# Two-layer trunk: FFN output blocks one by one in the first two parts, and the weight sums of a later pair queued behind a pair's second recombination

## The chip, the cores and the metric

The kernel runs on one core of a Trainium2 chip. The metric is the device time of one execution in microseconds (us). TensorE (PE) multiplies matrices into eight PSUM banks; VectorE (DVE), ScalarE (ACT) and GpSimd (POOL) do the element-wise work; SyncE (SP) issues most of the loads. PEld is TensorE's weight load, which runs beside its matmuls.

## The reference

512 tokens of width 1024 pass through two layers. A layer has a half-step SwiGLU feed-forward (FFN), a token mixer (retention in the first layer, forgetting attention in the second), a second half-step FFN and a gated per-layer embedding:

```
def swiglu(x, w_in, w_out):
    g, u = jnp.split(x @ w_in, 2, axis=-1)      # w_in: 1024 x (2*2816)
    return (jax.nn.silu(g) * u) @ w_out         # w_out: 2816 x 1024

h = h + 0.5 * swiglu(rmsnorm(h, nw[0]), ffn_w_in[i, 0], ffn_w_out[i, 0])
h = h + mixer(rmsnorm(h, nw[1]))
h = h + 0.5 * swiglu(rmsnorm(h, nw[2]), ffn_w_in[i, 1], ffn_w_out[i, 1])
h = h + sigmoid(rmsnorm(h, nw[3]) @ ple_w_gate[i]) * (p[i] @ ple_w_proj[i])
```

Everything is float32. The change touches the four FFNs alone.

## The kernel before

**Precision.** A float32 operand is split into a high part in TensorE's fp32r format and a low part, the remainder. A product takes three matmuls: high x high, high x low, low x high (lines L323, L324 and L325 for tiles of 512 tokens; L508 in `product`). For a weight block ScalarE casts the high part (L83) and VectorE subtracts for the low part (L84). For some blocks ScalarE casts and also writes the negated block (L125, L126), and a load of GpSimd's queue adds the block to it in memory (L127).

**FFN input.** A hidden block is 128 of the 2816 gate columns and the same of the up columns; there are 22 in an FFN. Most are made by a scheme of seven half-size products, on a `Pair` of weight tiles q and r of 512 KB each. r and q are added in four combinations (`emit_sums_now`, adds at L157: s1 to s4), each of which is split like a weight (tiles s12 and s34; a12 is a half of r, and `x` in the code). The pair's products go into two banks g and u:

- `one`: 24 matmuls of 128x256. `two`: 12 more, and a recombination: ScalarE copies g (L561), VectorE adds it to u (L562), ScalarE copies the sum (L564, called u2 in the code), VectorE adds that to g (L565).
- `three`: 48 matmuls. The first 12 need the copy of L564, the next 12 the sum of L565, the last 12 the a12 tile.
- `finish`: a copy (L578), two adds (L579, L580), and the gate: L585, Silu at L586, L590, and the split of the result (L313, L314) into the activation `act[m]`.

The first two or three blocks of an FFN are made without this scheme (`plain`). The others run in three parts, hidden blocks 0 to 5, 6 to 13 and 14 to 21. In a part the loop begins pair m + 1 (`start`, `one`, `two`) ahead of `three` and `finish` of pair m. At a part's end the first pair of the next part is begun; then the part's activations are multiplied with the output weights.

**FFN output.** `out_blocks` makes output blocks of 128 of the 1024 columns. Each takes 18 or 24 matmuls of 128x512 (three for each of the part's 6 or 8 hidden blocks). Then VectorE scales the bank (L604) and adds it to the residual stream `hall` (L607). Blocks 0 and 1 are made together, with their matmuls in turns; blocks 2 to 7 singly.

**What sets the order.** TensorE's order is the order of the code. A scheduler orders VectorE, ScalarE, GpSimd and SP. `issue_after` gives it one constraint: an instruction has to stand behind another one on the same engine. Weights are loaded and split ahead of use, through four raw buffers (`wraw`) and three split ones (`w8`, shown as w); the begun pair's q keeps one of the three during the output blocks. Sums are made for pairs up to two ahead of the number of pairs taken (`ahead`, `pairs_used`): before, `take_pair` counted a pair and asked for the sums at `start`.

## Time and profile before

| | |
|---|---|
| three runs, us | 2182.68, 2182.79, 2186.28; median 2182.79 |
| the profiled execution | 2182.19 us, of which the span is 2180.4 |
| DMA traffic | 268.40 MB, mean 123 GB/s |
| FFN0, FFN1, FFN2, FFN3 in the span, us | about 20 to 358, 767 to 1119, 1179 to 1505, 1761 to 2090 |

A row of a timeline has the start in us, the duration in us, engine, line, operation, output tile <- input tiles, shape and how many; in brackets the engine's idle time just before it, and the engine, tile and line whose work ended that idle time. A row of waits has the waiting engine, tile and line, what it waited for, the us in total, the number of waits and the longest. The ends of TensorE's matmuls are modelled; the distance between starts is the better measure of its pace.

### The profile page before, as it was taken

To read this page: it belongs to the slowest core of one execution; us is meant where nothing else is said; L and a number is where in the kernel's file an instruction comes from. 1 tells how busy PE (TensorE), PEld (TensorE's weight loads), DVE (VectorE), ACT (ScalarE), POOL (GpSimd) and SP (SyncE) were. 2 spreads that over 40 slices of the span, in tenths; PEclk is the share of its full clock that TensorE was granted. 3 is DMA by queue.
4 is the path that set the end of the run, shared out by engine and by line. 5 is a ranking of instruction groups with operands and counts; after the bars stand their busy time and mean duration, and the time that the engine had idled before them with its cause. 6 is when DMAs were issued, how large, how long until landed. Compare 5 with 4: busy or idle time off the path is not lost.

```text
span 2180.4 us, 34464 instructions
## 1 busy us (share of the span) xinstructions
PE 2138.2 (98%) x13537; PEld 1925.9 (88%) x13537; DVE 1446.2 (66%) x2627; ACT 1201.6 (55%) x2022; POOL 443.0 (20%) x344
## 2 busy tenths in 40 slices
PE   9999999999999999999999999999999999999997
PEld 9898987888888798989989999998788898999987
DVE  9776766352533677767758687775675686867765
ACT  8464553433333574746557565465786774655544
POOL 0010103444344000101110011012234200100055
PEclk9999999999999999999999999999999999999999
DMA  6464563222222244746526465564522144655631
GB/s 192 114 175 131 141 155 97 83 93 78 95 79 87 78 128 133 173 113 159 146 93 156 125 164 150 139 152 115 147 83 92 67 119 121 167 144 140 155 106 40
DMA packets 85603, 268.40 MB, mean 123 GB/s; under 512 B 9392, under 2 KB 12976, under 8 KB 85440
## 3 DMA queue, kind: packets, MB, share of 16 engines
q1 hardware_dynamic: 63328, 209.78, 29.0%
q0 software_dynamic: 20880, 55.32, 15.1%
q8 instruction: 106, 1.74, 0.3%
q10 hardware_dynamic: 1232, 1.09, 0.1%
q14 instruction: 57, 0.47, 0.1%
HBM read 264.02 MB, written 2.13 MB: 122 GB/s over the span
## 4 chain that ended last, share of the span: by engine, by line
PE 83%; DVE 6%; ACT 5%; DMA 3%; issue 2%; POOL 0%; SPq 0%; DVEq 0%; ACTq 0%; POOLq 0%
PE bank L508 31%; PE bank L325 14%; PE bank L323 14%; PE bank L324 14%; PE bank L543 3%; DMA wraw<-in_ffn_w_in 3%; PE bank L710 2%; PE bank L711 2%; PE bank L712 2%; DVE w L84 1%; ACT p L1014 1%; DVE tlo L314 1%; ACT w L83 1%; ACT p L1016 1%; DVE sums L157 1%
## 5 line engine op out<-in xcount | busy, mean ns | idle before, releaser
L83 ACT CAST w<-wraw 128x1024 fp32r<-128x1024 f32 (+1 forms) x238 | 241.5, 1022 | 421.6 <-PE bank L325 260.3
L325 PE MATMUL bank<-unit_a,w 128*128 128x512 f32 x736 | 287.0, 390 | 4.3 <-DVE w L84 2.6
L323 PE MATMUL bank<-unit_a,w 128*128 128x512 f32 x736 | 288.4, 392 | 1.9 <-ACT w L83 1.6
L324 PE MATMUL bank<-unit_a,w 128*128 128x512 f32 x736 | 286.7, 390 | 0.2 <-DVE unit_a L314 0.2
L83 ACT CAST s<-sums 128x512 fp32r<-128x512 f32 x316 | 189.1, 617 | 152.4 <-DVE sums L157 104.2
L325 PE MATMUL bank<-unit_d,w 128*128 128x512 f32 (+1 forms) x712 | 267.7, 376 | 4.7 <-DVE w L84 4.7
L323 PE MATMUL bank<-unit_d,w 128*128 128x512 f32 (+1 forms) x712 | 268.7, 377 | 3.2 <-ACT w L83 1.5
L324 PE MATMUL bank<-unit_d,w 128*128 128x512 f32 (+1 forms) x712 | 267.8, 376 | 1.7 <-DVE unit_d L314 1.7
L84 DVE TENSOR_TENSOR s<-sums,s 128x512 fp32r<-128x512 f32 x316 | 211.8, 686 | 75.0 <-ACT s L83 74.8
L84 POOL TENSOR_TENSOR w<-wraw,w 128x1024 fp32r<-128x1024 f32 x83 | 201.4, 2429 | 232.5 <-ACT w L83 224.0
L127 POOL DMA_DIRECT2D a<-in_ffn_w_in x80 | 70.1, 876 | 645.5 <-ACT a L126 452.4
L84 DVE TENSOR_TENSOR w<-wraw,w 128x1024 fp32r<-128x1024 f32 (+1 forms) x155 | 183.1, 1186 | 22.5 <-ACT w L83 22.3
L508 PE MATMUL bank<-unit_b,s 128*128 128x256 f32 x872 | 184.1, 277 | 1.7 <-DVE bank L565 1.7
L604 DVE SCALAR_TENSOR_TENSOR tmp<-bank,rows 128x512 f32<-128x512 f32 x96 | 66.1, 690 | 169.6 <-PE bank L325 168.3
L508 PE MATMUL bank<-unit_d,s 128*128 128x256 f32 x1140 | 178.4, 276 | 0.0
L508 PE MATMUL bank<-unit_a,s 128*128 128x256 f32 x1224 | 170.4, 276 | 0.0
L325 PEld LDWEIGHTS bank<-unit_a,w 128*128 128x128 f32 x736 | 138.2, 188 | 35.2 <-DVE w L84 4.3
L323 PEld LDWEIGHTS bank<-unit_a,w 128*128 128x128 f32 x736 | 138.2, 188 | 32.2 <-ACT w L83 3.5
L324 PEld LDWEIGHTS bank<-unit_a,w 128*128 128x128 f32 x736 | 138.2, 188 | 28.3 <-DVE unit_a L314 0.5
L325 PEld LDWEIGHTS bank<-unit_d,w 128*128 128x128 f32 x712 | 134.2, 188 | 30.5 <-DVE w L84 6.6
L323 PEld LDWEIGHTS bank<-unit_d,w 128*128 128x128 f32 x712 | 134.2, 188 | 30.1 <-ACT w L83 3.2
L324 PEld LDWEIGHTS bank<-unit_d,w 128*128 128x128 f32 x712 | 134.2, 188 | 26.3 <-DVE unit_d L314 3.2
(295 smaller groups left out, 4802.7 us busy)
## 6 DMA issues: line engine op xcount, KB each, us to landing
wraw<-in_ffn_w_in SPq DMA_DIRECT2D x174, 512.0 KB, 4.4
wraw<-in_ffn_w_out SPq DMA_DIRECT2D x64, 512.0 KB, 4.7
w<-in_ffn_w_in POOLq DMA_DIRECT2D x57, 512.0 KB, 5.4
a<-in_ffn_w_in POOLq DMA_DIRECT2D x79, 256.0 KB, 6.2
wraw<-in_ffn_w_out SPq DMA_DIRECT2D x32, 384.0 KB, 3.8
wraw<-in_ret_qk SPq DMA_DIRECT2D x16, 512.0 KB, 3.5
wraw<-in_ret_v SPq DMA_DIRECT2D x16, 512.0 KB, 3.6
wraw<-in_ret_g SPq DMA_DIRECT2D x16, 512.0 KB, 3.5
```

Source lines behind the costliest of these rows:

```text
L83: self.nc.scalar.copy(hi, raw)
L84: self.low.tensor_tensor(out=lo, in0=raw, in1=hi.bitcast(F32), op=ALU.subtract)
L127: self.nc.gpsimd.dma_start(out=lo, in_=src, accum_op=ALU.add)
L323: nc.tensor.matmul(out, wh, xh, start=first, stop=False)
L324: nc.tensor.matmul(out, wh, xl, start=False, stop=False)
L325: nc.tensor.matmul(out, wl, xh, start=False, stop=last)
L508: add = lambda w, x, start, stop: nc.tensor.matmul(out, w, x, start=start, stop=stop, skip_group_check=True)
L543: nc.tensor.matmul(o[:, HALVES[t]], x[:, ks], y, start=k == t == q == 0, stop=k == KB - 1 and q == 2, skip_group_check=True,)
L604: nc.vector.scalar_tensor_tensor(out=t1, in0=o, scalar=-0.5, in1=n.r, op0=ALU.mult, op1=ALU.mult)
L710: nc.tensor.matmul(os[t], xh, wh[:, js], start=k == 0, stop=False)
L711: nc.tensor.matmul(os[t], xh, wl[:, js], start=False, stop=False)
L712: nc.tensor.matmul(os[t], xl, wh[:, js], start=False, stop=k == KB - 1)
```

## The change

It does two things. In the first two parts of each FFN the output blocks 0 and 1 are made one after the other; in the third part they stay together. And a pair is counted, and the sums of the pair two ahead are asked for, at the end of `two` instead of at `start`, with the constraint that VectorE's first add of these sums stands behind `two`'s last VectorE instruction.

```
-    def take_pair(self, pair):
-        self.take(pair)
+    def next_sums(self, behind):
         self.pairs_used += 1
+        self.behind = (behind,)
         self.emit_sums()
-        return pair
+        self.behind = ()
...
         def start(m):
-            live[m] = W.take_pair(ins[m]), bank(), bank()
+            W.take(ins[m])
+            live[m] = ins[m], bank(), bank()
...
             nc.scalar.copy(u2, u[:, c1])
-            nc.vector.tensor_tensor(out=g[:, c1], in0=g[:, c1], in1=u2, op=ALU.add)
+            last = nc.vector.tensor_tensor(out=g[:, c1], in0=g[:, c1], in1=u2, op=ALU.add)
             live[m] += (cc,)
+            W.next_sums(last)
...
-            for ms in ((0, 1), (2,), (3,), (4,), (5,), (6,), (7,)):
+            pair = [(0, 1)] if done == NF else [(0,), (1,)]
+            for ms in pair + [(m,) for m in range(2, KB)]:
                 out_blocks(c, ms)
```

Lines move: the recombination is L562, L563, L565 and L566 in the changed kernel (L561, L562, L564, L565 before), `finish` L580, L581, L582, L587, L588 and L592 (L578, L579, L580, L585, L586, L590), the output drain L606 and L609 (L604, L607).

VectorE's order in the steady run of FFN0's third part. `sums` are the additions of a pair two ahead, `s_...` the low halves of sums; before:

```order
L157 TENSOR_TENSOR sums<-wraw 128x512
L562 TENSOR_TENSOR bank<-bank,tmp 128x256
L314 TENSOR_TENSOR unit_d<-tmp,unit_d 128x512
L84 TENSOR_TENSOR s_3052<-sums,s_3052 128x512
L84 TENSOR_TENSOR s_2782<-sums,s_2782 128x512
L565 TENSOR_TENSOR bank<-bank,tmp 128x256
L84 TENSOR_TENSOR s_2919<-sums,s_2919 128x512
L157 TENSOR_TENSOR sums<-sums,wraw 128x512
L579 TENSOR_TENSOR bank<-bank,tmp 128x256
```

The same place after:

```order
L563 TENSOR_TENSOR bank<-bank,tmp 128x256
L314 TENSOR_TENSOR unit_d<-tmp,unit_d 128x512
L566 TENSOR_TENSOR bank<-bank,tmp 128x256
L157 TENSOR_TENSOR sums<-wraw 128x512
L84 TENSOR_TENSOR s_2826<-sums,s_2826 128x512
L84 TENSOR_TENSOR s_3096<-sums,s_3096 128x512
L84 TENSOR_TENSOR s_2963<-sums,s_2963 128x512
L157 TENSOR_TENSOR sums<-sums,wraw 128x512
L581 TENSOR_TENSOR bank<-bank,tmp 128x256
```

The first add of the sums, the one that waits for a load, moved from ahead of the recombination (L562, L565 before) to behind it (L563, L566 after). ScalarE at the same place after (the copies of `two` at L562 and L565, then the negated weights of a later pair):

```order
L588 ACTIVATE tmp<-tmp 128x512
L562 COPY tmp<-bank 128x512
L313 CAST unit_d<-tmp 128x512
L565 COPY tmp<-bank 128x256
L125 CAST w_3042<-wraw 128x1024
L126 ACTIVATE w_3042<-wraw 128x1024
```

Both copies stand ahead of the weights' casts there. ScalarE at the end of FFN0's first part, where the last pair's `two` is recombined; before:

```order
L561 COPY tmp<-bank 128x512
L564 COPY tmp<-bank 128x256
L83 CAST w_934<-wraw 128x768
L313 CAST unit_d<-tmp 128x512
L83 CAST s_726<-sums 128x512
L83 CAST s_811<-sums 128x512
L578 COPY tmp<-bank 128x256
L125 CAST a_812<-wraw 128x512
L126 ACTIVATE a_812<-wraw 128x512
```

And after:

```order
L562 COPY tmp<-bank 128x512
L83 CAST s_852<-sums 128x512
L83 CAST s_853<-sums 128x512
L83 CAST w_934<-wraw 128x768
L83 CAST s_770<-sums 128x512
L313 CAST unit_d<-tmp 128x512
L83 CAST s_855<-sums 128x512
L125 CAST a_856<-wraw 128x512
L126 ACTIVATE a_856<-wraw 128x512
L565 COPY tmp<-bank 128x256
L580 COPY tmp<-bank 128x256
```

The pair's second copy (L564 before, L565 after) moved from the place right behind the first copy to behind the casts of the sums and of a12. On TensorE only the matmuls of blocks 0 and 1 change places, in the first two parts; SP and GpSimd keep their order.

## The prediction

> **What bounds the kernel now.** I read the page first, then TensorE's list of waits, then its timeline around each wait in the four FFNs, then VectorE's and ScalarE's timelines at the same places.

> The page's span and busy shares, then four rows of TensorE's waits (total us, times, longest us):

> ```profile
> span 2180.4 us, 34464 instructions
> PE 2138.2 (98%) x13537; PEld 1925.9 (88%) x13537; DVE 1446.2 (66%) x2627; ACT 1201.6 (55%) x2022; POOL 443.0 (20%) x344
> ...
> PE bank L325 <- DVE w L84: 7.3, 9, 2.0
> PE bank L508 <- ACT tmp L564: 4.1, 4, 3.0
> PE bank L323 <- ACT w L83: 3.1, 8, 0.5
> PE bank L508 <- DVE bank L565: 1.7, 1, 1.7
> ```

> TensorE works 98% of the span, and the change takes no instruction away, so it can only win TensorE's idle time: some 42 us in all, of which the four rows are the waits at the two places that the change touches. One of the nine in the first row (2.0 us) is TensorE waiting in the tail of FFN3 and stays.

> **Part 1: single output blocks in the first two parts.** TensorE's timeline after the pair (0,1), in FFN0's first part (six k-blocks) and second (eight):

> ```profile
> 87.51 0.39 PE L325 MATMUL bank<-unit_d,w 128*128 128x512 f32 x1
> 88.14 0.50 PE L323 MATMUL bank<-unit_d,w 128*128 128x512 f32 x1 [0.25 <-ACT w L83]
> 88.48 0.40 PE L324 MATMUL bank<-unit_d,w 128*128 128x512 f32 x1
> 89.55 0.51 PE L325 MATMUL bank<-unit_d,w 128*128 128x512 f32 x1 [0.67 <-DVE w L84]
> 89.89 0.40 PE L323 MATMUL bank<-unit_d,w 128*128 128x512 f32 x1
> ...
> 201.83 0.39 PE L325 MATMUL bank<-unit_d,w 128*128 128x512 f32 x1
> 202.72 0.50 PE L323 MATMUL bank<-unit_d,w 128*128 128x512 f32 x1 [0.51 <-ACT w L83]
> 203.06 0.40 PE L324 MATMUL bank<-unit_d,w 128*128 128x512 f32 x1
> 204.13 0.50 PE L325 MATMUL bank<-unit_d,w 128*128 128x512 f32 x1 [0.68 <-DVE w L84]
> 204.47 0.39 PE L323 MATMUL bank<-unit_d,w 128*128 128x512 f32 x1
> ```

> Undisturbed, one matmul follows another after 0.227 us, so four steps take 0.91. From 87.51 to 89.89 they take 2.38: 1.47 lost, of which 0.92 is idle time in brackets and 0.55 a slower start after the two waits (0.27 each). From 201.83 to 204.47 it is 1.73. The waits list has eight such places (four FFNs, two parts): 3.1 + 7.3 - 2.0 = 8.4 us idle, and 8 x 0.55 = 4.4 for the starts: **12.8 us**.

> Why they wait: VectorE and ScalarE there (two answers), with the later single blocks behind:

> ```profile
> 87.25 1.37 DVE L604 SCALAR_TENSOR_TENSOR tmp<-bank,rows 128x512 f32<-128x512 f32 x2 [6.13 <-PE bank L325]
> 88.54 1.82 DVE L84 TENSOR_TENSOR w<-wraw,w 128x768 fp32r<-128x768 f32 x2
> ...
> 93.52 0.69 DVE L604 SCALAR_TENSOR_TENSOR tmp<-bank,rows 128x512 f32<-128x512 f32 x1 [1.95 <-PE bank L325]
> ...
> 94.85 0.95 DVE L84 TENSOR_TENSOR w<-wraw,w 128x768 fp32r<-128x768 f32 x1
> 97.59 0.69 DVE L604 SCALAR_TENSOR_TENSOR tmp<-bank,rows 128x512 f32<-128x512 f32 x1 [1.79 <-PE bank L325]
> ...
> 87.25 1.57 ACT L83 CAST w<-wraw 128x768 fp32r<-128x768 f32 x2 [6.59 <-PE bank L325]
> ```

> Both blocks of the pair finish together, so both weight buffers come free together. Block 2's cast and subtraction begin only then, and VectorE first drains two banks. Blocks 3 to 7 already run alone with the same buffers: block 3 ended at 93.52, the low half of the buffer that it freed was rewritten by 94.85 + 0.95 = 95.80, and the block after next wanted it at 97.59, when block 4 ended: 1.8 us to spare. With singles, blocks 0 and 1 each have 18 matmuls (93.52 to 97.59: 4.07 us), or 24 in the second part (5.44); the cast, drain and subtraction take 2.3 us after a block by these rows (some 0.4 more at 1024 columns). So block 2's weights come over a block early: gain 12.8, bounds 0 and 12.8; I take 12.8, because those single blocks wait nowhere.

> A single block 0 reaches its last k-block sooner. The last activation's low half, and TensorE's first output matmul:

> ```profile
> 78.42 0.69 DVE L314 TENSOR_TENSOR unit_d<-tmp,unit_d 128x512 fp32r<-128x512 f32 x1 [0.69 <-ACT unit_d L313]
> ...
> 79.55 0.40 PE L323 MATMUL bank<-unit_d,w 128*128 128x512 f32 x1
> ```

> It is written at 79.11; a single block asks for it 15 matmuls after 79.55, at 82.95: 3.8 us of cover, so no cost. Nothing is added: as many matmuls, casts, drains and loads, and the SP and GpSimd queues keep their order.

> **Part 2: the weight sums behind two's second recombination.** The waits of TensorE on `two`, in all FFNs, and the granted clock after the longest (us; PE, PEld, DVE, ACT, POOL busy; PEclk):

> ```profile
> 55.85 0.85 PE L508 MATMUL bank<-unit_b,s 128*128 128x256 f32 x5 [1.69 <-DVE bank L565]
> ...
> 279.90 1.69 PE L508 MATMUL bank<-unit_a,w 128*128 128x256 f32 x12 [0.41 <-ACT tmp L564]
> 292.87 1.83 PE L508 MATMUL bank<-unit_a,w 128*128 128x256 f32 x12 [3.04 <-ACT tmp L564]
> ...
> 1045.41 0.51 PE L508 MATMUL bank<-unit_b,w 128*128 128x256 f32 x2 [0.41 <-ACT tmp L564]
> ...
> 2039.01 0.50 PE L508 MATMUL bank<-unit_b,w 128*128 128x256 f32 x2 [0.25 <-ACT tmp L564]
> ...
> 294.50:299.00 4.50, 4.50 (x28) 4.50 (x28) 4.40 (x9) 2.18 (x5) 0.87 (x1) 0.65 0.94 221
> ```

> Third parts: 0.41 + 3.04 + 0.41 + 0.25 = 4.1 idle, 4 x 0.27 for the starts, and 4.50 x (1 - 0.65) = 1.6 at the low clock: **6.8 us**. FFN0's first part: 1.69 + 0.27 = 1.96.

> The low clock is a cost of the long wait. [...] In the trace the clock was 1.00 before that wait and 0.65 after it, so the measurement decides.

> Where the third parts' waits come from (VectorE's and ScalarE's timelines; the last two rows are from the chain of waits):

> ```profile
> 264.42 0.69 DVE L157 TENSOR_TENSOR sums<-wraw 128x512 f32<-128x512 f32 x1 [3.54 <-DMA wraw<-in_ffn_w_in]
> ...
> 275.74 0.69 DVE L157 TENSOR_TENSOR sums<-wraw 128x512 f32<-128x512 f32 x1 [1.35 <-DMA wraw<-in_ffn_w_in]
> ...
> 288.72 0.69 DVE L157 TENSOR_TENSOR sums<-wraw 128x512 f32<-128x512 f32 x1 [3.02 <-DMA wraw<-in_ffn_w_in]
> 289.33 0.42 DVE L562 TENSOR_TENSOR bank<-bank,tmp 128x256 f32<-128x256 f32 x1
> ...
> 292.46 0.36 ACT L564 COPY tmp<-bank 128x256 f32<-128x256 f32 x1
> ...
> 270.40 5.21 DMA wraw<-in_ffn_w_in
> ...
> 281.71 6.89 DMA wraw<-in_ffn_w_in
> ```

> VectorE waits for the r-weights of a pair two ahead and has L562 of the pair in hand queued behind. The rounds of this loop are 11.3 us (264.42 to 275.74) and 13.0 (to 288.72): from the sum to the next load's issue 6.0 (264.42 to 270.40), then 5.2 or 6.9 to landing. A pair costs TensorE 12.97 - 3.04 - 0.27 = 9.66 us (279.90 to 292.87, 84 matmuls; so `three`'s 48 take 5.5 and `one` and `two` 4.1). The loop is longer than the pair, so VectorE falls back each round until `two` is late.

> After the change L563 to L566 stand ahead of the sum, and ScalarE's copies of `two` (L562, L565) no longer lie between sum and a12 cast. Count from T0, the end of `three` of an earlier pair. VectorE and ScalarE have the rest of that pair's `finish` and then the recombination, eight dependent steps of 0.36 to 0.69 us (rows above and below), 4.0 in sum; with a handover of 0.1 to 0.2 each and one subtraction between, L566 is done at about T0 + 5.7. `three` of the same pair starts at T0 + 4.1 + 5.5 + 4.1 = 13.7, or at T0 + 9.6 where the part ends and no further pair is begun. That leaves 4 us at the least, and the r-load, now behind the recombination, can no longer hold it in its own round. From sum to the end of the a12 cast five steps remain, some 3.3 us; with the landing 8.5 to 10.2, about the pair's 9.66, so VectorE no longer falls back by more than 0.5 us a round. Queued behind the waiting sum are now the next `finish`'s L581 and L582, which TensorE meets only two pairs later. The step that is moved issues two loads besides: r on the SP queue (512 KB, the landings above) and the accumulating load of a12 on GpSimd's. Both queues keep their order; the second feeds `three`'s last product two pairs on. The sums themselves come later by some 3 us; they are wanted a pair period later still, so that costs nothing; were that cover gone, `one` would wait instead. I take 6.8; ends: 0 (the wait only moves) and 6.8.

> FFN0's first part differs: only three pairs, and the order shows ScalarE's u2 copy (L565) behind the casts of a12 (L125, L126). TensorE and ScalarE there before:

> ```profile
> 69.87 1.60 PE L508 MATMUL bank<-unit_a,w 128*128 128x256 f32 x12
> ...
> 70.07 0.62 ACT L125 CAST a<-wraw 128x512 fp32r<-128x512 f32 x1 [0.47 <-PE bank L508]
> 70.59 0.63 ACT L126 ACTIVATE a<-wraw 128x512 fp32r<-128x512 f32 x1
> ```

> Those casts wait for the end of the `three` before and start 0.20 us after the next `three` (69.87) could. With the wait at 55.85 gone, that point is 69.87 - 1.96 = 67.91. The casts then run from 68.11 to about 69.2, the copy to 69.55, and the last pair's `three` starts at 69.6 instead of 67.9. Of the 1.96 us, 1.7 come back as a new wait, and its start: net **0.2 us** won; ends 2.0 (no new wait) and -1 (VectorE's L566 later still).

> **Sum.** 12.8 + 6.8 + 0.2 = 19.8 us. The profiled execution took 2182.19 us (span 2180.4 and 1.8 around it), 0.6 below the median of the runs, 2182.79. 2182.2 - 19.8 = 2162.4; against the median **2163.0 us**, 0.9% faster. Within 0.2% (4.4 us) I call it no change; about that is what a measurement of this kernel can tell.

> **Rivals.**
> 1. *Only the output blocks win.* The loads stay late (up to 6.9 us here), VectorE falls back as before, and the third parts wait at `finish` or at another copy. For it: the loop with a late landing (10.2) is still over the pair's 9.66, and the new order binds VectorE only, so ScalarE can still put casts first, as in FFN0's first part. Against: in the third part's order the copy L565 stands ahead of L125. 2182.8 - 12.8 - 0.2 = 2169.8.
> 2. *Only the sums win.* Single blocks wait at 0 or 1 in place of 2, since a lone block asks for its second weights after 4.1 us. Against: the 1.8 us to spare above. 2182.8 - 6.8 - 0.2 = 2175.8.
> 3. *Slower: a new wait at the end of every part.* There `three` of the last pair follows the one before with only its 5.5 us between, and what I expect in FFN0's first part (1.7 + 0.27 = 1.97) would come at all twelve ends, since VectorE reaches L566 only after a sum that a late load holds. Eleven more at 1.97 are 21.7 us: 2184.7, no change. From 2.2 us each, (19.8 + 4.4) / 11, it is slower; at the longest such wait in the trace, 3.04 + 0.27, it is 36.4 us: 2199. Against: the 4 us of slack above, against landings at most 1.7 us apart (5.2 and 6.9). [...]

> **Chances.** The forecast 0.58 (2161 to 2165, by FFN0's ends). Rival 1 0.20, since the loop is near the pair's time. Rival 2 0.08. Part-end waits: no change 0.05, slower 0.05. More than forecast (other small waits go too) 0.04. So faster 0.90, same 0.05, slower 0.05. The range 2159 to 2173 holds the forecast, rival 1 and mixtures between them.

> **What would show it.** Part 1 right: no wait of L323 or L325 on w behind block 1, and L606 of blocks 0 and 1 a block apart. Part 2 right: no wait of L508 on L565 or L566 in the third parts, no clock dip near 295, L563 at VectorE before the sum's wait for its load. FFN0: a wait of some 1.7 us on L565 near 68. Wrong if L508 waits at each part's end, or if L323 waits for w at block 1.

## The result, and the profile after

The changed kernel took 2166.36 us in the median of its first six runs, against 2181.49 us before (six runs): a ratio of 0.9932, with a 95% interval of 0.9921 to 0.9944. Two later sets beside the kernel before gave 0.9921 (0.9908 to 0.9935) and 0.9929 (0.9917 to 0.9941). Over all sets the mean of 17 runs is 2165.5 us, that of 39 runs before 2181.5: 16.0 us less (standard error 0.6), where 19.8 were forecast. The profiled execution of the changed kernel took 2164.15 us, 18.0 less than the profiled one before.

The page of the changed kernel, and the rows of TensorE's waits that answer to those of before:

```profile
span 2162.4 us, 34445 instructions
PE 2131.9 (99%) x13537; PEld 1925.9 (89%) x13537; DVE 1454.0 (67%) x2627; ACT 1205.3 (56%) x2022; POOL 444.2 (21%) x344
...
PE bank L325 <- DVE w L84: 2.0, 1, 2.0
...
PE bank L508 <- ACT tmp L565: 1.5, 1, 1.5
```

Of the four rows of before, L323's wait for w and L508's for the add are gone. L325's has one wait left, the one in FFN3's tail; L508's wait on two's second copy has gone from four places to one, and that one is new.

VectorE where blocks 0 to 2 of FFN0's first part now run singly:

```profile
83.74 0.69 DVE L606 SCALAR_TENSOR_TENSOR tmp<-bank,rows 128x512 f32<-128x512 f32 x1 [2.73 <-PE bank L325]
84.47 0.69 DVE L609 TENSOR_TENSOR hall<-hall,tmp 128x512 f32<-128x512 f32 x1
85.08 0.95 DVE L84 TENSOR_TENSOR w<-wraw,w 128x768 fp32r<-128x768 f32 x1
87.82 0.69 DVE L606 SCALAR_TENSOR_TENSOR tmp<-bank,rows 128x512 f32<-128x512 f32 x1 [1.79 <-PE bank L325]
```

Block 0 ends at 83.74, the low half for block 2 is written at 85.08 + 0.95 = 86.03, and block 2 starts when block 1 ends, at 87.82: 1.8 us to spare, where TensorE had lost 1.5 us.

VectorE in FFN0's third part, around three successive rounds:

```profile
257.42 0.42 DVE L563 TENSOR_TENSOR bank<-bank,tmp 128x256 f32<-128x256 f32 x1
258.19 0.69 DVE L314 TENSOR_TENSOR unit_d<-tmp,unit_d 128x512 fp32r<-128x512 f32 x1 [0.35 <-ACT unit_d L313]
258.80 0.42 DVE L566 TENSOR_TENSOR bank<-bank,tmp 128x256 f32<-128x256 f32 x1
259.14 0.68 DVE L157 TENSOR_TENSOR sums<-wraw 128x512 f32<-128x512 f32 x1
...
268.86 0.68 DVE L157 TENSOR_TENSOR sums<-wraw 128x512 f32<-128x512 f32 x1
...
278.59 0.68 DVE L157 TENSOR_TENSOR sums<-wraw 128x512 f32<-128x512 f32 x1
```

The rounds are 9.72 and 9.73 us, TensorE's time for a pair, where they had been 11.3 and 13.0, and no bracket stands at L157. Over the whole kernel VectorE's waits for r fell from 58.7 us to 7.8; its row before and after:

```profile
DVE sums L157 <- DMA wraw<-in_ffn_w_in: 58.7, 43, 3.5
...
DVE sums L157 <- DMA wraw<-in_ffn_w_in: 7.8, 8, 1.6
```

TensorE has no wait behind the eight that are left.

TensorE, ScalarE and VectorE at the new wait, the end of FFN0's first part:

```profile
67.89 0.28 PE L508 MATMUL bank<-unit_c,a 128*128 128x256 f32 x1
69.66 1.58 PE L508 MATMUL bank<-unit_a,w 128*128 128x256 f32 x11 [1.50 <-ACT tmp L565]
...
68.20 0.62 ACT L125 CAST a<-wraw 128x512 fp32r<-128x512 f32 x1 [0.68 <-PE bank L508]
68.72 0.62 ACT L126 ACTIVATE a<-wraw 128x512 fp32r<-128x512 f32 x1
69.25 0.35 ACT L565 COPY tmp<-bank 128x256 f32<-128x256 f32 x1
...
68.20 0.42 DVE L563 TENSOR_TENSOR bank<-bank,tmp 128x256 f32<-128x256 f32 x1
```

The copy stands behind the two a12 casts, which start when TensorE has freed their buffer at the end of the `three` before. It also needs VectorE's first add, and that came only at 68.20, behind the sums of another pair. So the casts are not all of the wait: right behind the add the copy would have ended at about 69.0 instead of 69.60 (an estimate from these rows). That is some 0.6 of the 1.76 us lost; the rest is the late add.

Both traces have all 13,537 matmuls, so each matmul's start after can be set against the same one's before. What TensorE gained, stage by stage:

| where | gained, us |
|---|---|
| after the pair (0,1), eight places | 1.50, 1.76, 1.51, 1.73, 1.49, 1.76, 1.50, 1.76; together 13.0 |
| third parts, waits on `two` and the half clock near 295 | 5.64 in FFN0, 0.67 in FFN1, 0.51 in FFN3; together 6.8 |
| FFN0's first part | 1.98 + 0.12 - 1.76 = 0.3 |
| 364 to 369 us, a half clock that before did not have | -1.63 |
| the rest (the start, a load of the forgetting attention) | about -0.5 |
| the whole span | 18.0 |

### The profile page after: what moved, and what is told of

Same layout as the page of the kernel before. It is cut to its first block, busy times and chain, and to the rows that moved or that the text cites. A ratio compares the mean times of both kernels' runs of the same rounds, so it can differ in the third digit from the quotient of the medians.

```text
span 2162.4 us, 34445 instructions
## 1 busy us (share of the span) xinstructions
PE 2131.9 (99%) x13537; PEld 1925.9 (89%) x13537; DVE 1454.0 (67%) x2627; ACT 1205.3 (56%) x2022; POOL 444.2 (21%) x344
## 4 chain that ended last, share of the span: by engine, by line
PE 89%; DVE 4%; ACT 4%; issue 2%; DMA 1%; POOL 0%; SPq 0%; DVEq 0%; ACTq 0%; POOLq 0%
PE bank L508 35%; PE bank L323 14%; PE bank L324 14%; PE bank L325 14%; PE bank L543 4%; PE bank L713 2%; PE bank L714 2%; PE bank L715 2%; ACT p L1017 1%; DVE tlo L314 1%; ACT w L83 1%; DVE w L84 1%; ACT p L1019 1%; PE bank L337 0%; DMA wraw<-in_ffn_w_in 0%
## 5 line engine op out<-in xcount | busy, mean ns | idle before, releaser
L83 ACT CAST w<-wraw 128x1024 fp32r<-128x1024 f32 (+1 forms) x238 | 242.5, 1022 | 425.2 <-PE bank L325 257.8
L323 PE MATMUL bank<-unit_a,w 128*128 128x512 f32 x736 | 288.7, 392 | 0.3 <-DVE tmp L1051 0.3
L325 PE MATMUL bank<-unit_a,w 128*128 128x512 f32 x736 | 287.1, 390 | 1.7 <-POOL w L84 1.7
L324 PE MATMUL bank<-unit_a,w 128*128 128x512 f32 x736 | 287.4, 390 | 0.2 <-DVE unit_a L314 0.2
L83 ACT CAST s<-sums 128x512 fp32r<-128x512 f32 x316 | 185.7, 618 | 159.6 <-PE bank L508 89.5
L323 PE MATMUL bank<-unit_d,w 128*128 128x512 f32 (+1 forms) x712 | 268.2, 377 | 1.6 <-DVE unit_b L317 0.6
L324 PE MATMUL bank<-unit_d,w 128*128 128x512 f32 (+1 forms) x712 | 267.6, 376 | 1.8 <-DVE unit_d L314 1.8
L325 PE MATMUL bank<-unit_d,w 128*128 128x512 f32 (+1 forms) x712 | 267.1, 375 | 2.0 <-DVE w L84 2.0
L84 DVE TENSOR_TENSOR s<-sums,s 128x512 fp32r<-128x512 f32 x316 | 208.8, 686 | 65.8 <-ACT s L83 65.0
L84 POOL TENSOR_TENSOR w<-wraw,w 128x1024 fp32r<-128x1024 f32 x83 | 202.6, 2444 | 232.7 <-ACT w L83 222.6
L84 DVE TENSOR_TENSOR w<-wraw,w 128x1024 fp32r<-128x1024 f32 (+1 forms) x155 | 183.6, 1185 | 27.5 <-ACT w L83 27.4
L508 PE MATMUL bank<-unit_b,s 128*128 128x256 f32 x872 | 183.1, 276 | 0.0
L508 PE MATMUL bank<-unit_d,s 128*128 128x256 f32 x1140 | 178.3, 276 | 0.0
L606 DVE SCALAR_TENSOR_TENSOR tmp<-bank,rows 128x512 f32<-128x512 f32 x96 | 66.1, 689 | 164.5 <-PE bank L325 163.2
L508 PE MATMUL bank<-unit_a,s 128*128 128x256 f32 x1224 | 170.0, 276 | 0.0
L325 PEld LDWEIGHTS bank<-unit_a,w 128*128 128x128 f32 x736 | 138.6, 188 | 31.2 <-POOL w L84 2.1
L323 PEld LDWEIGHTS bank<-unit_a,w 128*128 128x128 f32 x736 | 138.5, 188 | 29.5 <-DVE tmp L1051 0.5
L324 PEld LDWEIGHTS bank<-unit_a,w 128*128 128x128 f32 x736 | 138.6, 188 | 28.6 <-DVE unit_a L314 0.5
L323 PEld LDWEIGHTS bank<-unit_d,w 128*128 128x128 f32 x712 | 134.0, 188 | 27.0 <-ACT unit_d L313 1.4
L325 PEld LDWEIGHTS bank<-unit_d,w 128*128 128x128 f32 x712 | 134.1, 188 | 26.3 <-DVE w L84 2.2
L324 PEld LDWEIGHTS bank<-unit_d,w 128*128 128x128 f32 x712 | 134.1, 188 | 26.3 <-DVE unit_d L314 3.2
```

Source lines behind the costliest of these rows:

```text
L83: self.nc.scalar.copy(hi, raw)
L84: self.low.tensor_tensor(out=lo, in0=raw, in1=hi.bitcast(F32), op=ALU.subtract)
L323: nc.tensor.matmul(out, wh, xh, start=first, stop=False)
L324: nc.tensor.matmul(out, wh, xl, start=False, stop=False)
L325: nc.tensor.matmul(out, wl, xh, start=False, stop=last)
L508: add = lambda w, x, start, stop: nc.tensor.matmul(out, w, x, start=start, stop=stop, skip_group_check=True)
```

## The experiments

Gains below called "by TensorE's starts" are read in the same way, matmul against matmul. Times of different sets are compared with the kernel before in the same set.

**The changed kernel again.** No edit.

> The changed kernel once more, timed beside the kernel before and profiled anew. Its first profile has the eight waits after the pair gone (13.0 us by TensorE's starts, instruction against instruction), 6.8 us gone in the third parts, 0.3 in FFN0's first part, and 1.6 us lost again at 364 to 369 us, where TensorE ran at half clock after an unchanged wait of 1.70 us that had cost no clock before. Theory A: the clock dips by chance of phase after waits of 1.5 to 3 us, so the same kernel shows other dips in another execution; expected here: 14 to 19 us below the kernel before, and at 364 a dip or none. Theory B: the dip at 364 belongs to the changed kernel (what runs ahead of it decides); expected: a dip of 1.6 us at the same place again.

Ratio 0.9921 (0.9908 to 0.9935), median 2165.15 against 2183.03 us. The profile repeats every stage of the first to 0.4 us except the clock. The granted clock behind the unchanged wait near 364 (stretch, PE, PEld, DVE, ACT and POOL busy, PEclk, DMA share, GB/s), in the first profile:

```profile
358.00:363.50 5.50, 4.19 (x18) 2.95 (x17) 3.20 (x4) 2.00 (x2) 2.02 (x1) 1.00 0.00 0
364.40:368.40 4.00, 4.00 (x12) 3.10 (x12) 3.29 (x3) 1.21 (x2) 2.23 (x1) 0.57 0.59 178
```

and in the second, with the wait itself:

```profile
363.77 0.50 PE L325 MATMUL bank<-unit_a,w 128*128 128x512 f32 x1 [1.71 <-POOL w L84]
...
364.20:368.20 4.00, 4.00 (x19) 3.29 (x18) 3.38 (x4) 1.12 (x2) 2.32 (x1) 1.00 0.61 160
```

The wait is the same (1.70 and 1.71 us), the program is the same, and only one execution dips. Theory B, a dip that belongs to the changed kernel, falls. The mean granted clock of this execution was 0.998, against 0.996 in the first, which had a second dip, in FFN3's tail (from 2092.06 us, 1.5 us lost). It is 3.1 us shorter than the first, as much as the first's two dips cost.

**Only the single blocks.** The kernel before, with the new `pair` lines alone:

```
-            for ms in ((0, 1), (2,), (3,), (4,), (5,), (6,), (7,)):
+            pair = [(0, 1)] if done == NF else [(0,), (1,)]
+            for ms in pair + [(m,) for m in range(2, KB)]:
```

> Only the output blocks 0 and 1 singly in the first two parts; the sums asked for at start as before. Theory A (two independent parts): TensorE's starts show the eight waits gone, 13.0 us, and the waits at 55.85 and in the third parts as before (some 1.9 and 6.8 us); the time falls by 13 us, give or take 3 for clock dips. Rival: the single blocks also bring the loads forward, so that the third parts' waits shrink with them; then 15 to 20 us. Other rival: without the moved sums the wait goes to blocks 0 and 1; then under 6 us.

0.9941 (0.9928 to 0.9955), which is 12.9 us (9.8 to 15.7) of the 2183.03 of before in this set. By TensorE's starts the same eight gains, 1.49 to 1.76, 13.0 together, so the wait did not go to blocks 0 and 1. The waits on `two` stay, but not in their old sizes:

```profile
55.69 0.50 PE L508 MATMUL bank<-unit_b,s 128*128 128x256 f32 x2 [1.13 <-DVE bank L565]
...
286.67 1.58 PE L508 MATMUL bank<-unit_a,w 128*128 128x256 f32 x11 [0.92 <-ACT tmp L564]
...
1036.84 0.51 PE L508 MATMUL bank<-unit_b,w 128*128 128x256 f32 x2 [1.36 <-ACT tmp L564]
```

The one of 3.04 us in FFN0 is now 0.92; FFN1's grew from 0.41 to 1.36. One profile could not tell an effect of the single blocks from chance; the last experiment but one does.

**Only the moved sums.** The changed kernel with the old line of blocks, the edit above the other way round.

> Only the sums behind the second recombination; blocks 0 and 1 as a pair everywhere. Theory A: the waits on the copy and the add of two go in the third parts (6.8 us with the half clock near 295), 0.3 us net in FFN0's first part with a new wait of 1.5 us near 69, and the eight waits after the pair stay: 7 us below the kernel before, give or take 3 for clock dips. Rival: part of the third parts' gain came from the single blocks' earlier loads; then 1 to 5 us.

0.9978 (0.9967 to 0.999), which is 4.8 us (2.2 to 7.2). By TensorE's starts 6.8 us in the third parts and 0.3 in FFN0's first part, against the profile of before, with the eight waits after the pair unchanged:

```profile
PE bank L325 <- DVE w L84: 7.3, 9, 2.0
PE bank L323 <- ACT w L83: 3.1, 8, 0.5
...
PE bank L508 <- ACT tmp L565: 1.5, 1, 1.5
```

The two parts add up: 12.9 + 4.8 = 17.7 us, and both together gave 17.2 in the same set. The single blocks' 12.9 is what their profile says; the sums' 4.8 is under the 6.8 + 0.3 of theirs, though its interval just reaches it. It lies in the rival's 1 to 5 us as well. Against the rival speaks this profile, in which no wait on `two` is left in the third parts though the blocks run as a pair, and the next profile of the kernel before, below.

**FFN0's sums one pair later.** In `two`, for FFN0 alone, the sums asked for after pair 4 wait until after pair 5:

```
-            W.next_sums(last)
+            if i or m != 4:
+                W.next_sums(last)
+            if not i and m == 5:
+                W.next_sums(last)
```

> The changed kernel, but in FFN0's first part the sums of pair 6 (asked for after two of pair 4) are asked for only after two of pair 5, together with those of pair 7. Theory A: the new wait of 1.5 us at 69.7 exists because ScalarE's copy L565 of pair 5 stands behind the casts of pair 6's a12, which wait for a buffer that TensorE frees only at 68; with the sums later the copy is ahead of them and TensorE saves 1.7 us there, so 1.5 to 2 us below the changed kernel by TensorE's starts. Rival: the copy is late because VectorE is full there (L563 at 68.2 behind eight subtractions and adds); then the wait stays or comes back at one of pair 6, and the gain is under 0.5 us.

0.9906 (0.9891 to 0.9921), median of four runs 2161.74 us. TensorE gains 1.76 us at 70 us and keeps it through the FFNs; for a load of the forgetting attention it waits 2.1 us, against 1.4 in the changed kernel. VectorE and ScalarE there:

```profile
62.66 0.43 DVE L563 TENSOR_TENSOR bank<-bank,tmp 128x256 f32<-128x256 f32 x1 [0.76 <-PE bank L508]
...
63.13 0.37 ACT L565 COPY tmp<-bank 128x256 f32<-128x256 f32 x1 [0.57 <-DVE bank L563]
...
68.11 0.62 ACT L125 CAST a<-wraw 128x512 fp32r<-128x512 f32 x1 [0.93 <-PE bank L508]
```

The copy is done 4.6 us before the casts, and the wait is gone. But the run does not tell theory from rival: with the sums later, VectorE came to the first add at 62.66, where it had been 68.20. In the changed kernel both were late, the add because of the sums ahead of it on VectorE, the copy because of the casts.

**No constraint.** The sums asked for at the end of `two`, but free on VectorE:

```
-        self.behind = (behind,)
         self.emit_sums()
-        self.behind = ()
```

> The changed kernel with the sums still asked for at the end of two, but without the constraint that binds them behind two's last VectorE instruction. VectorE's order then has the waiting sum between L563 and L566 instead of behind L566; ScalarE's order is the same. Theory A: in the changed kernel VectorE waits nowhere for a load of r (43 waits and 58.7 us before, none after), since the loop of sum, casts and next load has become shorter than a pair; so a sum ahead of L566 costs nothing and the time is that of the changed kernel within 1.5 us by TensorE's starts (clock dips left out). Rival: it is the constraint that keeps late loads out of two's way; then waits of L508 on L565 or L566's lines come back in the third parts, 2 us or more.

0.9913 (0.9896 to 0.9929), median 2162.6 us. TensorE waits nowhere on `two`, in the third parts or at 70 us, where the 1.76 us are gained too. VectorE does wait for r again; a round, and the row of its waits (line numbers from L196 on are two lower in this kernel):

```profile
265.65 0.42 DVE L561 TENSOR_TENSOR bank<-bank,tmp 128x256 f32<-128x256 f32 x1
266.93 0.69 DVE L157 TENSOR_TENSOR sums<-wraw 128x512 f32<-128x512 f32 x1 [0.85 <-DMA wraw<-in_ffn_w_in]
267.54 0.68 DVE L312 TENSOR_TENSOR unit_d<-tmp,unit_d 128x512 fp32r<-128x512 f32 x1
268.14 0.43 DVE L564 TENSOR_TENSOR bank<-bank,tmp 128x256 f32<-128x256 f32 x1
...
DVE sums L157 <- DMA wraw<-in_ffn_w_in: 30.7, 37, 2.5
```

Theory A had it right that a sum ahead of the last add costs nothing, though not that VectorE would wait nowhere: it waits 30.7 us in 37 places, all of them covered (in the changed kernel 7.8 us in 8, not none). Nor is ScalarE's order the same. At the end of FFN0's first part the first add, the copy and the a12 cast are:

```profile
64.60 0.42 DVE L561 TENSOR_TENSOR bank<-bank,tmp 128x256 f32<-128x256 f32 x1
...
65.64 0.35 ACT L563 COPY tmp<-bank 128x256 f32<-128x256 f32 x1
...
68.45 0.62 ACT L125 CAST a<-wraw 128x512 fp32r<-128x512 f32 x1 [0.20 <-PE bank L506]
```

The gain of the third parts thus comes with the place in the program at which the sums are asked for, which lets the scheduler put L561 (the first add) and ScalarE's copies ahead of them; the constraint adds nothing there. In FFN0's first part the new wait comes with it: without it the add runs 3.6 us earlier and the copy ahead of the casts.

**The pair at 2 and 3.**

```
-            pair = [(0, 1)] if done == NF else [(0,), (1,)]
-            for ms in pair + [(m,) for m in range(2, KB)]:
+            blocks = ((0, 1), (2,), (3,)) if done == NF else ((0,), (1,), (2, 3))
+            for ms in blocks + ((4,), (5,), (6,), (7,)):
```

> The changed kernel with blocks 2 and 3 made together in the first two parts, in place of 0 and 1 before. Theory A (a pair asks for two weight buffers at once and frees two at once): two disturbances at each of the eight places, a wait for block 3's weights just after the pair starts (block 1's buffer comes free only then: cast, drain and subtraction of 2.3 us, less what TensorE can do with block 2: 1.5 to 2 us), and one like before's at block 4 (1.5 or 1.7 us): 25 to 30 us more than the changed kernel. Rival (the wait belongs to the start of the output stage, where loads and the last activations come late): single blocks 0 and 1 have passed that, so the pair costs under 5 us in all.

2197.12 us in one run. By TensorE's starts it lost, at each of the eight places, twice what the old pair lost once: 3.0 or 3.6 us, 26.4 together (in the rest to 33 are the clock, with a mean of 0.994 against 0.996, and a load of the forgetting attention, waited for 2.3 us instead of 1.4). TensorE at the pair's start and after its end, in FFN0's first part:

```profile
90.87 0.51 PE L323 MATMUL bank<-unit_d,w 128*128 128x512 f32 x1 [0.29 <-ACT w L83]
92.28 0.50 PE L325 MATMUL bank<-unit_d,w 128*128 128x512 f32 x1 [0.68 <-DVE w L84]
99.86 0.50 PE L323 MATMUL bank<-unit_d,w 128*128 128x512 f32 x1 [0.25 <-ACT w L83]
101.26 0.51 PE L325 MATMUL bank<-unit_d,w 128*128 128x512 f32 x1 [0.66 <-DVE w L84]
```

So the wait goes with the pair, not with the start of the output stage; and a pair that follows a single block pays at both ends.

**Every r loaded twice.** One line behind the load of r:

```
             raw = self.load(pair.r)
+            self.nc.sync.dma_start(out=raw, in_=pair.r)
```

> The changed kernel with every r loaded twice into the same tile, one load after the other, so that its landing takes some 9 to 10 us instead of 4 to 7; nothing else is left out. Theory A: the loop of sum to next load (3.3 us) and landing is then some 13 us, longer than the pair's 9.7, so VectorE waits for r again (waits of L157 on its load, none in the changed kernel), falls back some 3 us a pair, and TensorE waits at two once a slack of 4 to 8 us in each part is used up: 50 to 250 us more in all. Rival: the loads have a far wider margin (they are issued early enough by the four raw buffers), and TensorE loses under 10 us.

2248.65 us in one run, 84 us more than the changed kernel by TensorE's starts. VectorE's rounds are 12.5 us (269.79 to 282.25), and TensorE waits for sums and copies (line numbers from L156 on are one higher in this kernel):

```profile
269.79 0.69 DVE L158 TENSOR_TENSOR sums<-wraw 128x512 f32<-128x512 f32 x1 [4.45 <-DMA wraw<-in_ffn_w_in]
...
282.25 0.69 DVE L158 TENSOR_TENSOR sums<-wraw 128x512 f32<-128x512 f32 x1 [3.82 <-DMA wraw<-in_ffn_w_in]
...
PE bank L509 <- DVE s L84: 27.9, 17, 2.4
PE bank L509 <- ACT tmp L566: 25.3, 15, 4.4
```

The loop of sum, casts and load is what sets the round as soon as it is longer than the pair. With the second load the round grew by 2.7 us, and VectorE waits 4.45 and 3.82 us for r at the start of two rounds. The margin is small: in the changed kernel the r-load for the sum at 268.86 landed at 268.56, only 0.3 us before VectorE came to it.

**The kernel before again.** No edit.

> The kernel before once more, for a second profile of it. Theory A: its eight waits after the pair are the same to 0.1 us, since nothing of them hangs on a load, while the waits on two's copies differ, since they hang on landings that accumulate: third parts of 2 to 6 us in place of the 5.2 us (idle and starts) of the first profile; and its clock dips stand at other places. Rival: the third parts' waits are as fixed as the others: 5.2 us again, to 0.3 us.

2178.18 us in one run. The eight waits after the pair are the same to 0.1 us. The waits on `two` are not:

```profile
55.55 0.86 PE L508 MATMUL bank<-unit_b,s 128*128 128x256 f32 x5 [1.24 <-DVE bank L565]
...
289.14 1.70 PE L508 MATMUL bank<-unit_a,w 128*128 128x256 f32 x12 [0.28 <-ACT tmp L564]
...
1040.37 0.51 PE L508 MATMUL bank<-unit_b,w 128*128 128x256 f32 x2 [0.77 <-ACT tmp L564]
...
2035.01 0.51 PE L508 MATMUL bank<-unit_b,w 128*128 128x256 f32 x2 [0.28 <-ACT tmp L564]
```

In the third parts 1.33 us idle, with the slower starts (0.27 each) 2.1, in place of 6.8; the wait of 3.04 us is not there, and the matmuls behind the 0.28 us in its place are 0.11 us apart (five in 0.56 us from 290.68), where behind the 3.04 us they were 0.21 apart. With the 3.1 us of the kernel with single blocks alone (2.34 idle and three starts), which has the same order around `two`, that makes three executions: 6.8, 2.1 and 3.1 us, mean 4.0, nearer to the 4.8 that the moved sums alone gave in the time than the 6.8 is. The wait shrank here without single blocks, so its new size there needs no effect of theirs. Its mean granted clock was 0.997, against 0.996 in the first profile.

**No constraint, and the changed kernel, once more.** No new edits.

> The changed kernel without the constraint, once more, to see whether its 1.76 us in FFN0's first part (no wait at 69.7) can be told in the time: expected 2161 to 2164 us, 1 to 3 us below the changed kernel timed beside it, with no wait of TensorE on two's copies. If the third parts' waits were absent by luck of the landings in its first profile, some return here (0.3 us or more on a copy of two); if the place of the request carries the gain, none does.

> The changed kernel a third time, beside the one without the constraint: 2164 to 2167 us, with the wait of 1.5 us on L565 at 69.7 and no wait of two's copies in the third parts; clock dips at places that differ from those of the two profiles so far.

Without the constraint 0.9917 (0.9904 to 0.9931), median 2164.38 us; the changed kernel 0.9929 (0.9917 to 0.9941), 2165.31. TensorE's starts are 1.76 us ahead at 70 us again, and no wait on `two` came back, so their absence was no luck. The time of this set does not tell the two apart: the medians are 0.9 us apart, where 1 to 3 were expected, and the intervals overlap. The changed kernel has its wait of 1.50 us at 69.63 again and none on `two` in the third parts; its mean granted clock was 0.996, as in the first profile, but 1.00 behind the wait near 364. Over all sets the version without the constraint has a mean of 2162.9 us (ten runs), 2.6 below the changed kernel (standard error 0.8), of which the stage accounts for 1.8.

## Why the prediction was right, and where not

The time fell inside the range and the sign was right. But 2166.36 us is above the 2161 to 2165 given for the forecast itself, and the range also held rival 1 (2169.8), so the time alone would not show that the mechanism was right. The traces do, step by step:

- *Single blocks, 12.8 us.* Right: 13.0 by TensorE's starts, with the moved sums and without, and 12.9 (9.8 to 15.7) in the time. The 1.8 us to spare, read from blocks 3 to 5 before, are the 1.8 at block 2 after. The mechanism (two buffers wanted and freed at once) was shown by moving the pair.
- *Activation and weights for a lone block 0.* Right: no wait at block 0 or 1.
- *The loop of r's load.* Right in kind: rounds of 11.3 and 13.0 became 9.7, VectorE's waits for r fell from 58.7 us to 7.8, and a longer landing brought the loop back at 12.5. The 8.5 to 10.2 us that were forecast for the loop, "about the pair's 9.66", held: two rounds of the trace have 8.9 and 9.4 from sum to the r-load's landing. So the loop stayed close to the pair's time, as the eight waits that are left show. Rival 1, in which the loop would stay too long, did not come.
- *The third parts, 6.8 us.* The failed step, and it is one of size. The prediction summed the waits of one execution; they hang on landings and on a clock dip, and were 6.8, 2.1 and 3.1 us in three executions of that order. With a mean of 4.0 in its place, and none for FFN0's first part (below), the sum is 16.8 instead of 19.8; the 16.0 over all sets lies 0.8 below that, under two of its standard errors. The 1.6 us for the clock belonged to that one execution as well. The profiles bear out that the dip belongs to the long wait: 2.01 of its 3.04 us lay in the 3.41 us right ahead of the dip (last section); in the changed kernel's first profile, without that wait, the clock was 1.00 from 240 to 300 us, and in the kernel before again, with 0.28 us there, the matmuls behind kept full pace.
- *Who carries it.* Half of the reason was superfluous. The prediction rested on L563 to L566 standing ahead of the sum; without the constraint the last add stands behind it and TensorE still does not wait.
- *FFN0's first part, 0.2 us.* Right, 0.3: a wait of 1.50 us at 69.66 where 1.7 near 69.6 was forecast. The cause named (the a12 casts ahead of the copy) is a part of it, some 0.6 us. The prediction did not reckon with the first add, L563, coming at 68.20; that its sum came out all the same is partly luck, since casts and add were late by nearly as much. In the two kernels without the wait both the add and the copy come earlier. The 0.3 belongs to one execution too: in the two others of the old order the wait near 55.6 was 1.24 and 1.13 instead of 1.69, and the change would have lost 0.1 and 0.2 there, so over the three it wins nothing.
- *Part ends (rival 3).* Did not come: no wait at the other eleven ends.
- *What was not in the sum.* A half clock behind an unchanged wait cost 1.63 us in the profiled execution after and nothing in the next.

What stays open: three executions are few for a mean of the third parts' waits, and the time alone (4.8, from 2.2 to 7.2) does not tell 4.0 from 6.8. The runs of one kernel scatter by 1.8 us (the 17 after) and 2.5 (the 39 before), one standard deviation, and most of it goes with the clock. The changed kernel's eight runs with a mean granted clock of 0.995 average 2166.9 us, the six at 0.996 2164.9, the two at 0.997 2163.7, and the one at 0.998 took 2161.1; one dip, 3.41 us at half clock, is 0.0008 of the clock's mean. How much of FFN0's new wait each engine causes was not tested by a run that moves only one of them.

## What to carry to other kernels

When two blocks share a rotation of few buffers and run in turns, they free their buffers together, and the next block pays for the refill (here 1.5 to 1.8 us at each of eight places); the trace of blocks that already run singly tells what a change to singles will give. A stall that hangs on a load's landing had a different size in each execution here (6.8, 2.1 and 3.1 us): take its price from several profiles, or give it bounds down to a third. A constraint on one engine's order should be checked against the other engines' order at the first and last rounds of a loop; here the place in the program did the work in the third parts, and the new wait came with the constraint. When a run removes a wait, look at everything that moved: here ScalarE's copy and VectorE's add had both come earlier.

## What the runs showed of the hardware that was not expected

In the changed kernel's first profile TensorE's clock halved for 3.41 us (364.92 to 368.33 us: matmuls 0.427 us apart in place of 0.227; 1.62 us lost) after an idle time of half that, and it did not do so each time. Behind the same wait of 1.70 us at 364 the granted clock was 0.57 in the first profile of the changed kernel and 1.00 in the two others, and it was 1.00 behind the same 1.70 us in the kernel before (372.89 us).

The first profiles of the two kernels have four such dips; besides, the clock was 0.50 in the last 8.8 and 8.9 us of their spans. Each of the four is 3.41 us long at 0.50, and the idle time of TensorE ahead of it was:

| kernel | wait, us | its end | the dip's start | TensorE busy in the 3.41 us ahead of the dip |
|---|---|---|---|---|
| before | 3.04 | 292.87 | 294.27 | 1.40 |
| before | 2.04 | 2109.04 | 2110.16 | 1.37 |
| changed | 1.70 | 363.89 | 364.92 | 1.71 |
| changed | 2.02 | 2090.73 | 2092.06 | 1.40 |
